# Attention products with V in one block per head, the sums by ones in another PSUM bank, and eleven query rows for every second key tile

## The chip, the cores and the metric

The kernel runs on one core of a Trainium2 chip. Its time is the device time of one execution in microseconds (us). Five engines work side by side, each through its own instructions in order, and wait for each other by semaphores: PE (TensorE, matrix products into PSUM), DVE (VectorE), ACT (ScalarE), POOL (GpSimd) and SP (which only issues DMAs here).

## The reference

One layer of a diffusion backbone on 1024 latent tokens, a grid of 16 rows and 64 columns, with 256 context tokens and a width of 1024. A modulated RMS norm is followed by one input projection. Half of its columns feed a neighbourhood attention of 8 heads of 64, the other half a gated short convolution. An output projection and a gated residual end the layer. What concerns the change is the attention:

```python
def neighbourhood_attention(q, k, v, kc, vc, rpb):
    ...
    wh = min(WIN_H, rows)                                    # 8 of 16 rows
    row_start = jnp.clip(qi - wh // 2, 0, rows - wh)
    row_idx = row_start[:, None] + jnp.arange(wh)[None, :]
    ...
    col_start = jnp.clip(cols - WIN_W // 2, 0, GRID_W - WIN_W)   # 16 of 64 columns
    ...
    s_lat = jnp.where(col_valid[:, None, :], s_lat, -jnp.inf)    # q_rot . k_rot * scale + bias
    s_ctx = jnp.einsum('biqhd,blhd->bhiql', q_plain, kc, ...) * scale
    s = jnp.concatenate([s_lat.reshape(*s_lat.shape[:4], n_lat), s_ctx], axis=-1)
    p = jax.nn.softmax(s, axis=-1).astype(v.dtype)
    o = (jnp.einsum('bhiqrk,birkhd->biqhd', p_lat, v_rows)
         + jnp.einsum('bhiql,blhd->biqhd', p_ctx, vc))
```

A query in row i sees the key rows from clip(i - 4, 0, 8) on, eight of them. So the keys of rows 0 to 7 are seen by query rows 0 to 11, and the keys of rows 8 to 15 by query rows 5 to 15.

## The kernel before

**Stages.** The norm and the modulation come first, then the projection of q, k and v by pairs of heads (PSUM tiles `pacc`), then the attention, and last the output projection (`pout`). The projections of the gates and of the convolution (`pu`) are cut into *ticks* of six 128x512 matmuls, and the attention uses them as a filling between its own work: 136 ticks in all, most of them in the attention.

**Key tiles and quarters.** A head's 1024 keys are 8 tiles of 128 (8 rows by 16 columns): tile j holds column group j // 2 and row half j % 2. A *quarter* is the pair of tiles 2g and 2g + 1, so a head has four, and the whole attention 32, numbered n = 4 h + g. Scores lie with the keys on the partitions and the queries along the row. A tile sees the query columns `span(j)`, which are 24, 31, 31 and 23 columns for g = 0 to 3, and by `seen` 12 query rows: 0 to 11 for even tiles, 4 to 15 for odd ones. `cells` cuts the same columns from the packed copy of the scores.

**One step of the loop**, `quarter(n)`, writes in this order:
- DVE: adds quarter n - 4's exponentials of the context keys to the head's running sums (`ctx_sum`) and quarter n - 5's of the latent keys (`lat_sum`, two instructions, one for each tile); then up to three chores of the filling.
- PE: the scores of quarter n into `sbank`, a tile of two PSUM banks (`pss`); the scores of the context keys of quarter n + 1 (`pc`), and between its two halves the transposes that bring maxima back to rows (`pmx<-ci,rm`).
- DVE adds the bias (`sb<-pss,bt`), which frees `sbank`; subtracts the maxima from quarter n - 3; ACT takes the exponentials.
- PE: one tick of filling, the transposes of the maxima of quarter n - 2 (`pmx<-ci,mx`), DVE's reduction of them (`rm`).
- PE, when o = n - 4 is the first quarter of a head or the last of all: the *block* of products with V (`weighted`), for the quarters since the last block, which are quarters 1, 2, 3 of one head and quarter 0 of the next. Then `total`: the head's sums over the partitions, as products with a column block of ones, into columns 384 to 511 of both banks of `sbank`.
- DVE: running maxima (`ctx_max`, `lat_max`); PE: the remaining ticks; ACT, after a block: `finish`, which copies the sums and the head's output out of PSUM and issues their DMAs.

The number of ticks of each step stands in the table `TICKS`, 36 numbers.

**The block.** An output `po` is one PSUM bank: partitions 0 to 63 hold the head's 64 channels for query columns 0 to 31, partitions 64 to 127 for columns 32 to 63. A product of V (128 keys by 64) with exponentials goes into one of the two halves; the two lists of products, one for each half, are issued alternately, wide ones first. A tile whose columns cross 32 is cut into two pieces. Per head each half has four latent products that are wide (288 or 276 columns), two narrow ones (96 or 84) and four of 256 columns with the context keys. `po` comes from the PSUM tag "O" with two buffers.

**What sets the order.** In the attention every engine's instructions are chained in the order in which the program writes them. After it the chaining ends (`strict[:] = []`), and a scheduler orders the loads, splits and matmuls of the output projection.

The lines that issue a block and the sums before:

```python
if live(o) and (o % 4 == 0 or final):
    weighted([m for m in range(o - 2 - (o % 4 == 0), o + 1) if live(m)])
    if o:
        hd_ = heads[(o - 1) // 4]
        hd_.total()
```

Of the kernel before, what the change touches and what calls it, by code (L numbers as in the profile page):

```python
# [19 lines left out]
P = 128  # L20
# [35 lines left out]
def body(tc, es, x, xb, xt, cb_, ct, w_mod, w_gate, b_ada, w_grp, w_col, q_g, k_g, bias, w_out, vecs, cst, out):  # L56
# [779 lines left out]
    def span(j):  # L836

        return max(j // 2 * 16 - 7, 0), min(j // 2 * 16 + 24, GW)

    def seen(v, j, cols=None):  # L840

        lo, hi = cols or span(j)
        return v.rearrange("p (c r) -> p c r", r=16)[:, lo:hi, 4 * (j % 2):4 * (j % 2) + 12]

    def cells(v, j, cols=None):

        at = span(j)
        lo, hi = cols or at
        return v[:, (lo - at[0]) * 12:(hi - at[0]) * 12].rearrange("p (c r) -> p c r", r=12)

    class head:
        def __init__(self, h):
# [45 lines left out]
            self.cps[g] = sc  # L898

        def scores(self, j, ps):  # L900
            q = seen(self.q[:, 0], j)
            for l in range(2):
                pe.matmul(cells(ps, j), self.k[:, j // 2, l, j % 2 * P:(j % 2 + 1) * P], q, start=(l == 0), stop=(l == 1))

        def lat_max(self, j, sb):
            m = seen(mx[:], j)
# [29 lines left out]

        def total(self):

            for i in range(2):
                for b in range(4):  # L940
                    at = 256 * b + 128 * i
                    pe.matmul(sbank[32 * b:32 * b + 32, i, 384:], onef, self.sum[:, at:at + 128], start=True, stop=True, skip_group_check=True)

        def finish(self):

            sums = ap.tile([P, 256], F32, name="sums", tag="sums", bufs=1)
            act.copy(sums[:].rearrange("p (r i c) -> p i r c", i=2, c=8), sbank[:, :, 384:].rearrange("p i (c r) -> p i r c", r=16))
            act.dma_start(rs_d[self.p][self.s].rearrange("b (x c) -> (b x) c", c=256),
                          sums[:].rearrange("(x o) c -> x o c", o=32)[:, 0])
            ob = ap.tile([P, 512], F32, name="ob", tag="ob", bufs=1)  # L950
            act.copy(blocked(ob[:]), self.po.rearrange("p (b c r) -> p b r c", b=2, r=16))
            for bank in range(2):
                act.dma_start(o_d[self.p][64 * self.s:64 * self.s + 64, bank * 512:(bank + 1) * 512], ob[64 * bank:64 * bank + 64])

    def pair_of(n):

        h, g = divmod(n, 4)
        return [(a, heads[h], 2 * g + a) for a in range(2)] if 0 <= h < NH else []
# [34 lines left out]
                     pm[:, 256:256 + nb * P].rearrange("p (i k) -> p i k", i=nb))  # L993
        return back

    def weighted(quarters):

        sides = [], []
        for m in quarters:
            for i, hd_, j in pair_of(m):  # L1000
                if j == 0:
                    hd_.po = psm.tile([P, 512], F32, name="po", tag="O", bufs=2)[:]
                for piece in hd_.pieces(j, sbs[m][:, i]):
                    sides[piece[0]].append((hd_, *piece))
            hd_ = heads[m // 4]
            for piece in hd_.ctx_pieces(m % 4):
                sides[piece[0]].append((hd_, *piece))
        for bank, side in enumerate(sides):
            side.sort(key=lambda piece: -piece[-1].free_size())
        for k in range(max(map(len, sides))):  # L1010
            for bank, side in enumerate(sides):
                if k < len(side):
                    hd_, _, j, dst, src = side[k]
                    pe.matmul(dst, hd_.v[:, j], src, start=(hd_, bank) not in opened, stop=k == len(side) - 1,
                              skip_group_check=True)
                    opened.add((hd_, bank))

    opened = set()

    def quarter(n):  # L1020

        live = lambda m: 0 <= m < 4 * NH
        ticks = TICKS[n]
        e, o = n - 3, n - 4
        final = o == 4 * NH - 1
# [24 lines left out]

        def biased():
            sb = sbs[n] = sb_new()
            bt = now[0][1].bt[:].rearrange("p v n -> p (v n)")[:, :1128].rearrange("p (a n) -> p a n", a=2)
            for at, slot, w_ in (((0, 31, 8), (8, 15, 16)), ((0, 0, 31),), ((0, 0, 31),), ((0, 0, 15), (15, 39, 8)))[n % 4]:
                dve.tensor_tensor(sb[:, :, at * 12:(at + w_) * 12], sbank[:, :, at * 12:(at + w_) * 12],
                                  bt[:, :, slot * 12:(slot + w_) * 12], ALU.add)

        if now and n >= 2:
            biased()
        if live(e):  # L1060
            heads[e // 4].ctx_exp(e % 4)
            w = both(sbs[e], e)
            w4 = w.rearrange("p a (c r) -> p a c r", r=12)
            dve.tensor_tensor(w4, w4, maxima_of(e), ALU.subtract)
            act.activation(w, w, AF.Exp)
        for _ in range(n > 0):
            next(fill, None)
        if 0 < n and n - 2 < 4 * NH:
            backs.append(maxima(n - 2))
        done = []  # L1070
        if live(o) and (o % 4 == 0 or final):
            weighted([m for m in range(o - 2 - (o % 4 == 0), o + 1) if live(m)])
            if o:
                hd_ = heads[(o - 1) // 4]
                hd_.total()
                done.append(hd_)
                if hd_.s:
                    ready.append(hd_.p)
# [347 lines left out]
```

## Time and profile before

| | before |
|---|---|
| median of 3 runs (lowest, highest) | 610.72 us (608.78, 611.19) |
| profiled execution, its own time | 609.24 us |
| its span | 607.5 us |
| mean granted clock of PE | 0.996 |
| PE busy | 594.1 us, 98% of the span |
| DVE, ACT, POOL busy | 401.5, 273.5, 66.3 us |
| from 258 to 502 us, the attention | PE busy 241.54 of 244 us, DVE 207.38, ACT 123.10 |

A row of the timeline gives the start in us, the time from the first start to the last end of the merged instructions, the engine, the line, the operation, what it writes and reads, the shape, the count, and in brackets how long the engine was idle before and what released it. Since nearly all instructions are issued through helper functions, their line is L71, and the tile names tell the groups apart. The end of a matmul in the profile is modelled and overlaps the next one's start, so the pace of matmuls is read from start to start. A product of 32-bit values without rounding (all products with V and with ones) stands in the trace as two records.

### The profile page before, as it was taken

How to read it: one execution, taken by the hardware profiler on the slowest of the kernel's cores; microseconds unless marked ns; L12 is line 12 of the kernel's file. 1: busy time of each engine (PE TensorE's matmuls, PEld its weight loads, DVE VectorE, ACT ScalarE, POOL GpSimd, SP SyncE). 2: the span in 40 equal slices, each digit the busy share in tenths (PEclk: the TensorE clock that was granted, in tenths of full speed). 3: DMA queues.
4: the chain of work that ended last, by engine and by line, in shares of the span. 5: the costliest groups of instructions: out<-in, count | busy, mean ns of one | idle time of the engine just before them, and what ended most of it. 6: DMA issues, size and time to landing. Idle time of an engine off the chain costs nothing.

```text
span 607.5 us, 9599 instructions
## 1 busy us (share of the span) xinstructions
PE 594.1 (98%) x3412; PEld 503.7 (83%) x3412; DVE 401.5 (66%) x833; ACT 273.5 (45%) x636; POOL 66.3 (11%) x86
## 2 busy tenths in 40 slices
PE   7799999999999999999999999999999999999998
PEld 3577899999999999888878787878787778888887
DVE  1476879646536555468999787999897785493201
ACT  6645355426526446334464464556455545360000
POOL 1001024123213222000000000000000002003200
PEclk9899999999999999999999999999999999999999
DMA  8995566734424673956264646546732227953631
GB/s 325 413 417 202 179 233 195 235 114 151 156 88 153 222 259 120 327 192 212 71 215 152 229 149 235 172 167 219 234 112 82 81 70 219 373 172 117 230 104 53
DMA packets 63227, 116.14 MB, mean 191 GB/s; under 512 B 7377, under 2 KB 26313, under 8 KB 60876
## 3 DMA queue, kind: packets, MB, share of 16 engines
q1 hardware_dynamic: 56684, 103.95, 49.5%
q10 hardware_dynamic: 6240, 11.05, 5.9%
q0 software_dynamic: 256, 0.54, 0.3%
q8 instruction: 27, 0.44, 0.3%
q14 instruction: 20, 0.16, 0.1%
HBM read 86.08 MB, written 29.43 MB: 190 GB/s over the span
## 4 chain that ended last, share of the span: by engine, by line
PE 94%; DMA 3%; DVE 1%; SPq 1%; ACT 0%; issue 0%
PE pu L71 31%; PE pacc L71 21%; PE po L71 6%; PE acc L71 5%; PE pout L92 5%; PE pout L90 5%; PE pout L91 5%; PE pss L71 4%; PE cacc L71 4%; DMA slab<-in_w_mod 3%; PE pc L71 2%; PE pmx L71 2%; PE tr L71 1%; PE trA L71 1%; PE trB L71 1%; SPq L71 0%
## 5 line engine op out<-in xcount | busy, mean ns | idle before, releaser
L71 PE MATMUL pu<-h,uh 128*128 128x512 f32 x544 | 172.2, 398 | 0.0
L71 PE MATMUL pacc<-w,h 128*128 128x384 f32 x768 | 138.9, 337 | 0.9 <-ACT ub L71 0.5
L71 PEld LDWEIGHTS pacc<-w,h 128*128 128x128 f32 x768 | 132.7, 188 | 1.8 <-ACT ub L71 0.9
L71 PEld LDWEIGHTS pu<-h,uh 128*128 128x128 f32 x544 | 97.3, 188 | 18.3 <-issue 1.0
L71 PE MATMUL pu<-h,ul 128*128 128x512 f32 x272 | 106.5, 392 | 0.0
L71 PEld LDWEIGHTS pu<-h,ul 128*128 128x128 f32 x272 | 51.1, 188 | 11.4
L71 POOL TENSOR_TENSOR ss<-ss,few 128x4 f32<-128x4 f32 (+1 forms) x40 | 41.2, 1030 | 126.3 <-DVE ss L71 126.1
L91 PE MATMUL pout<-wol,yh 128*128 128x512 f32 (+2 forms) x136 | 51.6, 379 | 0.0
L92 PE MATMUL pout<-woh,yl 128*128 128x512 f32 (+2 forms) x136 | 50.4, 379 | 0.0
L90 PE MATMUL pout<-woh,yh 128*128 128x512 f32 (+2 forms) x136 | 50.4, 379 | 0.0
L71 PE MATMUL acc<-h,w 128*128 128x512 f32 x144 | 38.2, 411 | 0.0
L71 ACT COPY mg<-pmx 128x256 f32<-128x256 f32 (+1 forms) x33 | 12.1, 367 | 57.4 <-PE pmx L71 42.8
L71 DVE TENSOR_REDUCE ss<-sq 128x4 f32<-128x260 f32 (+1 forms) x40 | 15.7, 393 | 28.4 <-ACT sq L71 28.3
L71 DVE TENSOR_TENSOR sb<-pss,bt 128x192 f32<-128x192 f32 (+3 forms) x48 | 27.7, 604 | 10.1 <-PE pss L71 10.1
L71 PEld LDWEIGHTS acc<-h,w 128*128 128x128 f32 x144 | 26.6, 194 | 8.7 <-ACT h L71 1.2
L71 ACT ACTIVATE sq<-pacc 128x256 f32<-128x256 f32 x32 | 12.4, 387 | 47.2 <-PE pacc L71 46.5
L71 DVE TENSOR_TENSOR sum<-sum,sb 128x372 f32<-128x372 f32 (+2 forms) x64 | 31.9, 498 | 2.0
L71 DVE TENSOR_TENSOR mx<-mx,sb 128x372 f32<-128x372 f32 (+2 forms) x64 | 31.8, 497 | 1.9
L71 ACT ACTIVATE qn<-pacc,ss 128x64 f32<-128x64 f32 x128 | 30.1, 330 | 4.9 <-PE trA L71 2.5
L71 ACT ACTIVATE sc<-sc 128x512 f32<-128x512 f32 x32 | 20.2, 633 | 21.6 <-DVE sc L71 21.6
L71 DVE TENSOR_TENSOR ul<-uraw,uh 128x512 fp32r<-128x512 f32 x34 | 23.0, 684 | 10.5 <-ACT uh L71 10.5
L91 PEld LDWEIGHTS pout<-wol,yh 128*128 128x128 f32 x136 | 25.6, 188 | 4.7
(141 smaller groups left out, 939.6 us busy)
## 6 DMA issues: line engine op xcount, KB each, us to landing
uraw<-in_w_col SPq DMA_DIRECT2D x34, 256.0 KB, 3.5
slab<-in_w_mod SPq DMA_DIRECT2D x8, 1024.0 KB, 9.6
q_d<-qs SPq DMA_DIRECT2D x32, 256.0 KB, 2.2
k_s<-k_d SPq DMA_DIRECT2D x8, 1024.0 KB, 7.6
q_s<-q_d SPq DMA_DIRECT2D x16, 512.0 KB, 4.9
wr<-in_w_grp SPq DMA_DIRECT2D x40, 192.0 KB, 2.4
bt<-in_rpb SPq DMA_DIRECT2D x8, 564.0 KB, 6.9
xn<-in_xb SPq DMA_DIRECT2D x8, 512.0 KB, 8.2
```

Source lines behind the costliest of these rows:

```text
L71: i = emit(*a, **kw)
L90: i = pe.matmul(ps, ah, bh, start=first, stop=False)
L91: pe.matmul(ps, ah, bl, start=False, stop=False)
L92: pe.matmul(ps, al, bh, start=False, stop=last)
```

## The change

It has three parts and a new table.

1. `weighted` takes one whole head. A block is written where o is the *last* quarter of a head (n = 4 h + 7), and has this head's four quarters. The block of quarter 0 of the first head alone, which stood at n = 4, is gone; there are 8 blocks, before there were 9.
2. `total` writes to a tile `ptot` of its own from the tag "O", as four products of 256 columns, before eight of 128 columns into `sbank`. `finish` copies from it.
3. `seen` and `cells` give odd tiles 11 query rows (5 to 15) in the maxima, the sums and the products with V. The scores are computed on 12 rows as before (`twelve`).

Since a block needs all the sums of its head, `lat_sum` is called for two quarters in the step of a block, for none in the step after it, and for one in the others. `TICKS` moves the step with few ticks from n % 4 = 0 to n % 4 = 3; its sum is 110 as before.

```diff
-TICKS = [2, 3, 3, 3, 2, 4, 4, 3] + 2 * [1, 4, 4, 4] + [2, 4, 4, 4] + 2 * [1, 4, 4, 3] + [1, 4, 4, 2] + [1, 3, 4, 3]
+TICKS = [2, 3, 3, 4, 4, 4, 4, 1] + [4, 4, 4, 1] + [4, 4, 4, 2] + [4, 4, 4, 1] + 3 * [4, 4, 3, 1] + [3, 2, 3, 1]
...
     def seen(v, j, cols=None):
 
         lo, hi = cols or span(j)
-        return v.rearrange("p (c r) -> p c r", r=16)[:, lo:hi, 4 * (j % 2):4 * (j % 2) + 12]
+        return v.rearrange("p (c r) -> p c r", r=16)[:, lo:hi, 5 * (j % 2):12 + 4 * (j % 2)]
+
+    def twelve(v, j):
+
+        lo, hi = span(j)
+        return v.rearrange("p (c r) -> p c r", r=16)[:, lo:hi, 4 * (j % 2):12 + 4 * (j % 2)]
...
-        return v[:, (lo - at[0]) * 12:(hi - at[0]) * 12].rearrange("p (c r) -> p c r", r=12)
+        return v[:, (lo - at[0]) * 12:(hi - at[0]) * 12].rearrange("p (c r) -> p c r", r=12)[:, :, j % 2:]
...
         def total(self):
 
-            for i in range(2):
-                for b in range(4):
-                    at = 256 * b + 128 * i
-                    pe.matmul(sbank[32 * b:32 * b + 32, i, 384:], onef, self.sum[:, at:at + 128], start=True, stop=True, skip_group_check=True)
+            self.tot = psm.tile([P, 512], F32, name="ptot", tag="O", bufs=2)
+            for b in range(4):
+                pe.matmul(self.tot[32 * b:32 * b + 32, :256], onef, self.sum[:, 256 * b:256 * b + 256], start=True, stop=True, skip_group_check=True)
...
-    def weighted(quarters):
-
+    def weighted(hd_):
+
+        hd_.po = psm.tile([P, 512], F32, name="po", tag="O", bufs=2)[:]
         sides = [], []
-        for m in quarters:
-            for i, hd_, j in pair_of(m):
-                if j == 0:
-                    hd_.po = psm.tile([P, 512], F32, name="po", tag="O", bufs=2)[:]
+        for m in range(4 * hd_.h, 4 * hd_.h + 4):
+            for i, _, j in pair_of(m):
                 for piece in hd_.pieces(j, sbs[m][:, i]):
...
-        for m in (o - 1, o)[:1 + final]:
+        for m in () if o % 4 == 0 else (o - 1, o) if o % 4 == 3 else (o - 1,):
             for i, hd_, j in pair_of(m):
                 hd_.lat_sum(j, sbs[m][:, i])
...
-        if live(o) and (o % 4 == 0 or final):
-            weighted([m for m in range(o - 2 - (o % 4 == 0), o + 1) if live(m)])
-            if o:
-                hd_ = heads[(o - 1) // 4]
-                hd_.total()
-                done.append(hd_)
+        if live(o) and o % 4 == 3:
+            hd_ = heads[o // 4]
+            weighted(hd_)
+            hd_.total()
+            done.append(hd_)
```

How the instructions stand. First PE before, at n = 4, the short block of the first head's quarter 0 between two ticks:

```order
L71 MATMUL pu<-h_251,ul 128x512
L71 MATMUL pmx<-ci,mx 128x128 x2
L71 MATMUL po<-sb,v_3055 64x24x12 x2
L71 MATMUL po<-sc,v_3055 64x256 x2
L71 MATMUL pu<-h_164,uh 128x512 x2
```

All four products go to the same half, and in the changed program nothing stands in their place. Next PE before, at n = 8, the end of the first long block, with the sums and the scores that follow (v_3055 is the first head's V; the block began with its last three quarters and the second head's first one, v_3056, mixed by width):

```order
L71 MATMUL po<-sc,v_3055 64x256
L71 MATMUL po<-sb,v_3055 64x7x12
L71 MATMUL po<-sb,v_3055 64x8x12
L71 MATMUL po<-sb,v_3055 64x7x12
L71 MATMUL po<-sb,v_3055 64x8x12
L71 MATMUL pss<-sum,onef 32x128 x8
L71 MATMUL pss<-q_s,k_s 128x372 x4
```

The sums by ones and the scores behind them write the same tile `pss`. And PE in the changed program, the first head's block at n = 7, in full:

```order
L71 MATMUL pmx<-ci,mx 128x128 x2
L71 MATMUL po<-sb,v_3055 64x24x12 x2
L71 MATMUL po<-sb,v_3055 64x23x12 x2
L71 MATMUL po<-sb,v_3055 64x24x11 x2
L71 MATMUL po<-sc,v_3055 64x256 x8
L71 MATMUL po<-sb,v_3055 64x23x11 x2
L71 MATMUL po<-sb,v_3055 64x7x12
L71 MATMUL po<-sb,v_3055 64x8x12
L71 MATMUL po<-sb,v_3055 64x7x11
L71 MATMUL po<-sb,v_3055 64x8x11
L71 MATMUL ptot<-sum,onef 32x256 x4
L71 MATMUL pss<-q_s,k_s 128x288 x4
```

As many products as before stand in the block, from one head, half of the latent ones narrower by a twelfth; scores follow the sums directly in both, before the second quarter of the same head (372 columns), now the first of the next (288). Last, DVE in the changed program at n = 11, around the start of the step of a block:

```order
L71 TENSOR_TENSOR mx<-mx,sb 128x31x11
L71 TENSOR_TENSOR sum<-sc 128x256
L71 TENSOR_TENSOR sum<-sum,sb 128x31x12
L71 TENSOR_TENSOR sum<-sum,sb 128x31x11
L71 TENSOR_TENSOR sum<-sum,sb 128x23x12
L71 TENSOR_TENSOR sum<-sum,sb 128x23x11
L71 TENSOR_TENSOR ul<-uraw,uh 128x512
L71 TENSOR_TENSOR sb<-pss,bt 128x2x180
```

Four sums over latent keys stand ahead of the bias there, before it were two in every step. Behind the last sums by ones PE has 60 matmuls `pu` (10 ticks) in the changed program and 66 (11 ticks) before; up to the first step of the attention, the instructions of every engine stand as they did.

More of the change, by code (lines that the diff above doesn't have):

```diff
@@ L900, in scores @@
         def scores(self, j, ps):
-            q = seen(self.q[:, 0], j)
+            q = twelve(self.q[:, 0], j)
             for l in range(2):
-                pe.matmul(cells(ps, j), self.k[:, j // 2, l, j % 2 * P:(j % 2 + 1) * P], q, start=(l == 0), stop=(l == 1))
+                pe.matmul(cells(ps, j - j % 2), self.k[:, j // 2, l, j % 2 * P:(j % 2 + 1) * P], q, start=(l == 0), stop=(l == 1))
         def lat_max(self, j, sb):
@@ L994, in maxima @@
         return back
-    def weighted(quarters):
+    def weighted(hd_):
+        hd_.po = psm.tile([P, 512], F32, name="po", tag="O", bufs=2)[:]
         sides = [], []
-        for m in quarters:
-            for i, hd_, j in pair_of(m):
-                if j == 0:
-                    hd_.po = psm.tile([P, 512], F32, name="po", tag="O", bufs=2)[:]
+        for m in range(4 * hd_.h, 4 * hd_.h + 4):
+            for i, _, j in pair_of(m):
                 for piece in hd_.pieces(j, sbs[m][:, i]):
-                    sides[piece[0]].append((hd_, *piece))
-            hd_ = heads[m // 4]
+                    sides[piece[0]].append(piece[1:])
             for piece in hd_.ctx_pieces(m % 4):
-                sides[piece[0]].append((hd_, *piece))
-        for bank, side in enumerate(sides):
+                sides[piece[0]].append(piece[1:])
+        for side in sides:
             side.sort(key=lambda piece: -piece[-1].free_size())
[L1010 to L1018, printed above, removed]
+        last = len(sides[0]) - 1
+        for k in range(last + 1):
+            for side in sides:
+                j, dst, src = side[k]
+                pe.matmul(dst, hd_.v[:, j], src, start=k == 0, stop=k == last, skip_group_check=True)
     def quarter(n):
@@ L1024, in quarter @@
         e, o = n - 3, n - 4
-        final = o == 4 * NH - 1
         left = do_frees(1) + 2 if n > 2 else 3
@@ L1070, in quarter @@
         done = []
[L1071 to L1078 removed]
+        if live(o) and o % 4 == 3:
[3 more added lines that the diff above has]
+            done.append(hd_)
+            if hd_.s:
+                ready.append(hd_.p)
         if now:
```

2 lines of the change are left out of this document (1 added, 1 removed).

## The prediction

> **What bounds the kernel now.** I read the page first, then a table of busy time by stage, the list of waits, and the timeline of PE around three blocks.
>
> ```profile
> PE 594.1 (98%) x3412; PEld 503.7 (83%) x3412; DVE 401.5 (66%) x833; ACT 273.5 (45%) x636; POOL 66.3 (11%) x86
> ...
> PE 94%; DMA 3%; DVE 1%; SPq 1%; ACT 0%; issue 0%
> ```
>
> PE is busy for 98% of the span and carries 94% of the chain that ends last. The table by stage has the stretch, then the busy time of PE, PEld, DVE, ACT and POOL:
>
> ```profile
> 72.00:258.00 186.00, 186.00 (x1078) 178.12 (x1076) 112.06 (x282) 87.79 (x314) 46.89 (x51) 1.00 0.57 189
> 258.00:502.00 244.00, 241.54 (x1494) 196.16 (x1493) 207.38 (x405) 123.10 (x214) 0.27 (x4) 1.00 0.49 162
> 502.00:604.60 102.60, 102.59 (x471) 85.98 (x469) 42.90 (x68) 23.15 (x38) 13.64 (x14) 1.00 0.56 187
> ```
>
> From 72 us to the last matmul PE has no gap except 2.46 us in the attention (244 less 241.54). So a product less there shortens the kernel by its own time, and what DVE or ACT save is worth nothing until PE waits for them. The list of waits, asked for PE in this stage alone, has one row (us in all, times, the longest):
>
> ```profile
> PE pss L71 <- ACT sums L71: 2.5, 5, 0.5
> ```
>
> Five times the scores waited for ACT's copy of the sums, which lie in the same tile. The timeline of PE shows the short block, a tick behind maxima without a block, and the first long block:
>
> ```profile
> 281.62 0.38 PE L71 MATMUL pmx<-ci,mx 128*128 128x128 f32 x2
> 281.93 1.19 PE L71 MATMUL po<-sb,v 128*64 128x288 f32 x4
> 282.95 1.03 PE L71 MATMUL po<-sc,v 128*64 128x256 f32 x4
> 283.90 0.74 PE L71 MATMUL pu<-h,uh 128*128 128x512 f32 x2
> 284.48 0.40 PE L71 MATMUL pu<-h,ul 128*128 128x512 f32 x1
> ...
> 288.17 0.38 PE L71 MATMUL pmx<-ci,mx 128*128 128x128 f32 x2
> 288.31 0.71 PE L71 MATMUL pu<-h,uh 128*128 128x512 f32 x2
> 288.86 0.40 PE L71 MATMUL pu<-h,ul 128*128 128x512 f32 x1
> ...
> 308.15 2.12 PE L71 MATMUL po<-sb,v 128*64 128x288 f32 x16
> 310.10 1.90 PE L71 MATMUL po<-sc,v 128*64 128x256 f32 x16
> 311.83 0.50 PE L71 MATMUL po<-sb,v 128*64 128x84 f32 x8
> 312.26 0.64 PE L71 MATMUL pss<-sum,onef 128*32 128x128 f32 x16
> 313.39 0.95 PE L71 MATMUL pss<-q_s,k_s 128*128 128x372 f32 x4 [0.49 <-ACT sums L71]
> ```
>
> The reader is to see three things. The 16 records of 256 columns take 310.10 to 311.83, 1.73 us, and in the short block 4 of them take 0.95 us: in a long block the two halves run beside each other, in the short one, with everything in one half, they run one by one. So a long block costs its longer half: 2 records of each product, 8 x 256 columns in 1.73 us, 0.845 ns for a column. And the scores start 1.13 us after the sums.
>
> **The change part by part.** *The short block goes.* From its maxima to the next tick are 2.28 us (281.62 to 283.90); where no block stands there, it is 0.14 us (288.17 to 288.31). The first pair of the tick takes 0.58 us behind the block and 0.55 us behind maxima. PE saves 2.14 + 0.03 = **2.17 us**. Its products don't come back: the long blocks stay eight and as long as they were, since the last one was lopsided already and took the full time with 30 records, where the others have 40:
>
> ```profile
> 496.31 4.11 PE po L71 x30
> ...
> 500.99 15.19 PE pu L71 x66
> 516.17 1.59 PE pout L90 x7
> ```
>
> (This is the chain of waits in order of time; 308.15 to 312.26 is 4.11 us too.)
>
> *Eleven rows.* In each half of a block one product of 288 columns becomes 264, one of 276 becomes 253, and one of 96 becomes 88 (84 becomes 77 beside it): 55 columns less in the longer half. Twice, since each is two records, at 0.845 ns: 0.093 us a head, **0.74 us** in all. The price of a run of 11 columns, which starts at an odd place, no row shows. The nearest rows are the runs of 12 at a step of 16 (the 16 records of 288 and 276) against the unbroken 256. The former have (4 x 288 + 4 x 276) = 2256 columns in 1.95 us, 0.864 ns each with the block's start in them, 2% over the unbroken ones. I take no surcharge; the bounds are the whole 0.74 us lost (a run of 11 priced as 12) and, far on the other side, the odd products at twice their time, which is a rival below.
>
> The Trainium skill says on this, in "PSUM — Partial Sum Buffer", Specifications (TRN2), that PSUM has lines of 8 bytes and that any access pattern with gaps slows matmuls significantly. The runs of 12 have gaps too and pay the 2%; by the page the change would keep or raise that price, by the rows it loses nothing.
>
> *The sums by ones.* Eight products of 128 columns become four of 256. Column for column that is the same work, and I take 0. From the sums to a following tick is 0.57 us (below), so the bounds are a tenth of that either way for each head, 0.5 us in all.
>
> *The wait goes.* Where a tick follows the sums, the step is shorter:
>
> ```profile
> 484.06 0.64 PE L71 MATMUL pss<-sum,onef 128*32 128x128 f32 x16
> 484.63 0.73 PE L71 MATMUL pu<-h,uh 128*128 128x512 f32 x2
> ```
>
> 0.57 us against 1.13 us, five times: 5 x 0.56 = **2.80 us**. In the changed program the scores don't touch the tile of the sums, and what else they need is long there. The next head's K and Q are asked for one and two steps before the block's step, and no wait of PE for them is in the list. The bounds are 0 (another wait ends as late) and 2.80. `ptot` comes from the tag of `po`: two buffers for `po`, `ptot`, `po`, `ptot` in turn, so each finds one whose content was copied a whole head ago.
>
> *DVE's four sums.* In the step of a block two more sums stand ahead of the bias. Their price and the nearest deadline, in the tightest steady step that I find (DVE, then PE):
>
> ```profile
> 420.64 0.41 DVE L71 TENSOR_TENSOR mx<-pc,sc 128x256 f32<-128x256 f32 x1
> ...
> 422.13 0.92 DVE L71 TENSOR_TENSOR sum<-sum,sb 128x276 f32<-128x276 f32 x2
> ```
> ```profile
> 422.90 0.40 PE L71 MATMUL pc<-q_s,kc_s 128*128 128x256 f32 x2
> 423.13 0.38 PE L71 MATMUL pmx<-ci,rm 128*128 128x128 f32 x2
> ```
>
> The next context scores (422.90) need the buffer that the maximum at 420.64 reads until 421.05: 1.85 us of room. Two sums of 276 columns take 0.92 us, so 0.9 us stay. The step ahead of them has a lighter one before it (no sums of latent keys at all in the step behind a block), so DVE doesn't run up a debt. I take 0. If that cover were gone, each of the eight blocks would wait for what is missing, at most the 0.92 us.
>
> *DVE's narrower maxima and sums* save a twelfth of instructions like the 0.92 us pair on an engine that PE doesn't wait for: 0. *The moved ticks* are 110 before and after; 12 or so stand between blocks in both: 0.
>
> *The last stage.* One tick less lies between the last block and the output projection, 15.19 / 11 = 1.38 us. That is cover for the first loads of the last stage. What is late there first is the seventh column group's y: ACT rounds its second half and DVE takes the rest, and PE uses them:
>
> ```profile
> 522.56 0.63 ACT L1317 CAST yh<-tb 128x512 fp32r<-128x512 f32 x1 [4.60 <-DMA tb<-y_d]
> ```
> ```profile
> 523.22 0.69 DVE L1318 TENSOR_TENSOR yl<-tb,yh 128x512 fp32r<-128x512 f32 x1 [4.53 <-ACT yh L1317]
> ```
> ```profile
> 524.40 0.39 PE L90 MATMUL pout<-woh,yh 128*128 128x512 f32 x1
> ...
> 525.08 0.39 PE L92 MATMUL pout<-woh,yl 128*128 128x512 f32 x1
> ```
>
> Room is 524.40 - 523.19 = 1.2 us. But the loads hang on the ticks (ACT's queue stands behind the second-last unit of the filling, and behind the last convolution, both counted back from the start of the output projection), not on the block. I take 0, with 1.4 us as the bound.
>
> *Sum:* 2.17 + 0.74 + 2.80 = 5.71 us. The profiled execution took 609.24 us, its span 607.5 and 1.7 around it; it becomes 603.5. The median, 610.72, lies 1.5 above that execution, so I predict **605.0 us**. Its own range, from the bounds of the small terms and the spread of the three runs (608.78 to 611.19), is 603.2 to 606.8.
>
> **The rivals.**
>
> *The wait only changes its name.* The scores behind a block are now a head's first, and they or the maxima behind them could be held by something that ends as late as the copy did. For it: the five waits were 0.49 us, small enough to have hidden another. Against it: the list has no other row. The gain is then 2.17 + 0.74 = 2.91 us: 607.8.
>
> *DVE becomes the bound in the step of a block.* For it: DVE is busy for 207 of 244 us here, and the room was 1.85 us in a step of three ticks, which the new table keeps for the last heads. Against it: the light step behind. If DVE comes 0.92 us too late at seven blocks, 6.4 us, it takes all: 611.4, no change. If half of that, 608.2.
>
> *The last stage starves.* Up to 1.4 us at the first late load: 606.4. If ACT's queue is pushed back at more than one load, twice that, 607.8.
>
> *Rows of eleven are dear (slower).* Runs of 44 bytes that begin at a multiple of 4 bytes may cost PE or its writes more than the runs of 12 do. Per head and half the odd products have 264 + 253 + 88 = 605 columns; at twice the time that is 2 x 605 x 0.845 ns = 1.02 us, 8.2 us for eight heads. The change then ends at 605.0 + 8.2 = 613.2. It is slower than before from a surcharge of 5.71 / 8.2, 70%, on. Against it stands the 2% of the runs of 12. It is what the page on PSUM quoted above warns of, if the slowing there grows with the oddness of the run.
>
> *The change doesn't do what it says* can't be a rival: the order of instructions has the eight blocks, the narrower products and the sums in `ptot`.
>
> **How the numbers follow.** My forecast has 0.77; the wait that changes its name 0.07; DVE 0.06; the last stage 0.06; the dear rows of eleven 0.04. The bound of "no change" is 0.5%, 3.05 us, about what a measurement of this kernel can tell: faster is below 607.67, slower above 613.77. The forecast's range lies in faster nearly whole (0.75), of the last stage 0.05, of the wait and of DVE 0.02 each: 0.84. Slower takes a part of the rows of eleven and the spread of the measurements: 0.03. The rest, 0.13, is no change. The range that should hold the time 8 times in 10 goes from 602.8 to 607.9: the forecast's own, a little under it for the runs' spread, and up to the case of the wait and the last stage.
>
> **What would show it.** In the profile after: no wait of PE for ACT's copy of the sums, and 0.57 us or so from the sums to the scores; eight blocks of about 4.02 us (4.11 less 0.09), nothing of `po` before 290 us; PE's gap in the attention near zero, and the attention shorter by 5.7 us, while the stages before it are as long as they were. Odd products should take as much less as they have columns less, 11 of 12. What would make it wrong: an odd product as long as an even one or longer, a new wait of PE for DVE within a step behind a block, or PE idle between 515 and 530 us for y or the output weights.

## The result: slower by half a per cent, and the profile after

The changed kernel took 615.01 us (median of 5 executions, 613.38 to 615.36). The ratio to the kernel before is 1.0058, with a 95% interval of 1.0032 to 1.0084. A second measurement of the same kernel gave 613.15 us (12 executions) and 1.0044, 1.0028 to 1.0061. The forecast was 605.0 us and faster. The first profiled execution took 613.38 us, its span is 611.4.

The page of the changed kernel, PE's busy time and the chain that ended last:

```profile
PE 594.8 (97%) x3347; PEld 501.1 (82%) x3348; DVE 400.3 (65%) x833; ACT 273.1 (45%) x636; POOL 66.3 (11%) x86
...
PE 80%; DMA 7%; DVE 6%; ACT 3%; issue 2%; ACTq 1%; SPq 0%; POOL 0%; DVEq 0%; POOLq 0%
```

PE carried 94% of the chain before, now 80%. The busy times by stage (stretch; its length; PE, PEld, DVE, ACT and POOL busy) say where:

```profile
72.00:258.00 186.00, 185.56 (x1073) 177.54 (x1072) 113.24 (x284) 87.35 (x313) 46.86 (x51) 1.00 0.56 187
258.00:502.00 244.00, 238.94 (x1411) 193.25 (x1411) 205.31 (x406) 122.66 (x211) 0.27 (x4) 1.00 0.48 163
```

PE idles for 5.06 us from 258 to 502 us, before for 2.46. What for stands in its list of waits (us in all, times, the longest):

```profile
PE pmx L71 <- ACT mg L71: 4.2, 4, 1.9
...
PE pmx L71 <- DVE rm L71: 0.8, 1, 0.8
...
PE pu L71 <- ACT zs L71: 0.5, 1, 0.5
...
PE pout L90 <- ACT yh L1313: 0.2, 1, 0.2
```

The row of before, scores behind ACT's `sums`, is gone. The new first row is the transposes of the maxima (`pmx<-ci,mx`), behind ACT's copy `mg`, which takes maxima that were brought back to rows out of PSUM. The timeline of PE around the fifth head's block, the worst place (start, duration, what, idle before and releaser; heads are counted from 1 here and in the expectations):

```profile
423.11 1.62 PE L71 MATMUL po<-sb,v 128*64 128x288 f32 x12
424.55 1.90 PE L71 MATMUL po<-sc,v 128*64 128x256 f32 x16
426.28 0.91 PE L71 MATMUL po<-sb,v 128*64 128x253 f32 x12
427.12 0.64 PE L71 MATMUL ptot<-sum,onef 128*32 128x256 f32 x8
427.69 0.81 PE L71 MATMUL pss<-q_s,k_s 128*128 128x288 f32 x4
...
430.18 0.39 PE L71 MATMUL pu<-h,ul 128*128 128x512 f32 x1
432.47 0.44 PE L71 MATMUL pmx<-ci,mx 128*128 128x128 f32 x2 [1.90 <-ACT mg L71]
```

The two savings in these rows came as priced: the block takes 4.01 us (423.11 to 427.12), and the scores follow the sums by 0.57 us. Then the scores, the context scores and a tick run through, and the maxima of the next step wait 1.9 us.

What `mg` waited for is on ACT's own queue. First ACT in the changed kernel, then in the kernel before, both behind the block of the fifth head (ACTq rows are DMA issues):

```profile
427.83 0.37 ACT L71 COPY sums<-ptot 128x256 f32<-128x256 f32 x1 [0.82 <-PE ptot L71]
428.18 0.59 ACT L71 COPY ob<-po 128x512 f32<-128x512 f32 x1
429.69 0.53 ACTq L952 DMA_DIRECT2D rs_d<-sums  x1
430.60 1.35 ACTq L957 DMA_DIRECT2D o_d<-ob  x2
432.04 0.37 ACT L71 COPY mg<-pmx 128x256 f32<-128x256 f32 x1 [3.28 <-DMA rb<-ri_d]
```
```profile
430.10 0.37 ACT L71 COPY sums<-pss 128x256 f32<-128x256 f32 x1 [2.09 <-PE pss L71]
430.37 0.59 ACT L71 COPY ob<-po 128x512 f32<-128x512 f32 x1
430.50 0.53 ACTq L948 DMA_DIRECT2D rs_d<-sums  x1
431.13 1.67 ACTq L953 DMA_DIRECT2D o_d<-ob  x2
432.89 0.37 ACT L71 COPY mg<-pmx 128x256 f32<-128x256 f32 x1 [1.93 <-DVE sb L71]
```

Between the copies and `mg` stand `finish`'s three DMA issues. Before, the first left 0.13 us after the start of `ob`, and `mg` ended at 433.26, 0.14 us ahead of PE's transposes:

```profile
433.40 0.38 PE L71 MATMUL pmx<-ci,mx 128*128 128x128 f32 x2
```

In the changed kernel the first issue stood for a microsecond and a half and the others followed late, 4.2 us from `sums` to `mg` instead of 2.8. In the list of ACT's waits three of the seven blocks stand out, those of heads 3, 5 and 6, and the releaser is a DMA each time:

```profile
ACT mg L71 <- DMA y_d<-tb: 3.5, 1, 3.5
ACT mg L71 <- DMA rb<-ri_d: 3.3, 1, 3.3
...
ACT mg L71 <- DMA o_d<-ob: 2.1, 1, 2.1
```

Why a store of 4 KB should wait for other transfers is told by the instructions of the built program. Each DMA of SP and ACT tells of its landing by a semaphore of a set of eight that are handed out in turn (the trace has 50 DMAs on each of the eight), and a DMA that takes a semaphore waits until the DMA before it on that semaphore has landed, as a rule the one eight issues earlier. Here are the rows of SP and ACT (number on its engine, name, what it waits for) around the fifth head's block:

```
273 L867 DMA k_s_4869<-k_d3_86 128x1x2048 [waits DMAHW6_49]
274 L319 DMA uraw_4780<-in_w_col 128x512 [waits DMAHW7_49,DVE_49]
275 L530 DMA rb_4728<-ri_d1_96 64x512 [waits DMAHW0_49,DVE_49]
...
280 L881 DMA v0_3055<-v_d3_90 128x640 [waits DMAHW5_49,PE_49]

472 L952 DMA rs_d2_73<-sums_4718 4x256 [waits DMAHW6_49,Activation_49]
473 L957 DMA o_d2_59<-ob_4721 64x512 [waits DMAHW7_49,Activation_49]
474 L957 DMA o_d2_59<-ob_4721 64x512 [waits DMAHW0_49]
```

The store of the sums has the semaphore of the next head's K. SP's timeline and part 6 of the page (KB each, median us to landing) put times to it:

```profile
422.78 0.71 SPq L867 DMA_DIRECT2D k_s<-k_d  x1
```
```profile
k_s<-k_d SPq DMA_DIRECT2D x8, 1024.0 KB, 7.1
```

The trace has K's landing at 429.62, 6.8 us after its issue, and the store left at 429.69. The two issues behind it left 0.08 and 0.02 us after the landings of `uraw` and `rb`, which had the semaphore before them, and at head 3 the two stores of the output left 0.08 and 0.04 us after those of `rb` and `y_d`. Before, K was issued at 419.37 and ten DMAs ahead of the store, which followed one from 420.78; that had landed at 429.17, and the store left at 430.50. Of the 24 issues of the kernel before none left less than 0.2 us after the landing that it needed. The block moved a step ahead, into the landing of the next head's loads.

That is heads 3 and 5. At heads 1 and 6 PE waits too (0.5 and 0.7 us), but the landings that the issues needed were 5 to 18 us old. There one issue took long by itself: 1.08 us at head 1, as in the kernel before, and 1.41 us at head 6, where 0.46 to 0.61 us are usual; why isn't shown. It becomes a stall because the room is gone everywhere, as at head 4, where no issue is held or long. First the kernel before, then the changed one:

```profile
402.02 0.37 ACT L71 COPY sums<-pss 128x256 f32<-128x256 f32 x1 [2.15 <-PE pss L71]
404.23 0.37 ACT L71 COPY mg<-pmx 128x256 f32<-128x256 f32 x1 [1.35 <-PE pc L71]
405.31 0.38 PE L71 MATMUL pmx<-ci,mx 128*128 128x128 f32 x2
```
```profile
400.29 0.37 ACT L71 COPY sums<-ptot 128x256 f32<-128x256 f32 x1 [0.61 <-PE ptot L71]
402.50 0.37 ACT L71 COPY mg<-pmx 128x256 f32<-128x256 f32 x1 [1.35 <-PE pc L71]
402.93 0.44 PE L71 MATMUL pmx<-ci,mx 128*128 128x128 f32 x2
```

ACT needs 2.21 us from `sums` to `mg` in both. Before, `mg` ended 0.71 us ahead of PE's transposes, now 0.06 us ahead of transposes that just waited for it. The scores' wait of 0.56 us, which the change removed, was cover for ACT's three issues, and so was the longer first product of scores (372 columns, now 288).

### The profile page after: what moved, and what is told of

It reads as the page before. It is cut to its first block, busy times and chain, and to the rows that moved or that the text cites. A ratio compares the mean times of both kernels' runs of the same rounds, so it can differ in the third digit from the quotient of the medians.

```text
span 611.4 us, 9460 instructions
## 1 busy us (share of the span) xinstructions
PE 594.8 (97%) x3347; PEld 501.1 (82%) x3348; DVE 400.3 (65%) x833; ACT 273.1 (45%) x636; POOL 66.3 (11%) x86
## 4 chain that ended last, share of the span: by engine, by line
PE 80%; DMA 7%; DVE 6%; ACT 3%; issue 2%; ACTq 1%; SPq 0%; POOL 0%; DVEq 0%; POOLq 0%
PE pu L71 24%; PE pacc L71 21%; PE acc L71 5%; PE po L71 4%; PE pout L90 4%; PE pout L92 4%; PE pout L91 4%; PE cacc L71 4%; DMA rb<-ri_d 3%; PE pss L71 2%; PE tr L71 2%; PE pmx L71 2%; PE pc L71 2%; DMA woraw<-in_w_out 2%; DMA xn<-in_xb 1%
## 5 line engine op out<-in xcount | busy, mean ns | idle before, releaser
L90 PEld LDWEIGHTS pout<-woh,yh 128*128 128x128 f32 x136 | 25.6, 188 | 5.7 <-ACT yh L1313 1.1
L92 PEld LDWEIGHTS pout<-woh,yl 128*128 128x128 f32 x136 | 25.6, 188 | 5.1 <-DVE yl L1314 0.4
```

The lines of the kernel that those rows point to most:

```text
L90: i = pe.matmul(ps, ah, bh, start=first, stop=False)
L92: pe.matmul(ps, al, bh, start=False, stop=last)
```

## The experiments

All kernels are alike up to the first scores. These start anywhere from 257.3 to 261.4 us in the 14 profiles, the kernel before among the early ones at 258.0 (its issue with SP at 258.3). So beside the times the table has the stretch from the first scores to the end of the span, which leaves that chance out. That column is of one profiled execution each, and two of the changed kernel differ by 2.5 us in it; so differences of 1 us or less between kernels are read from steps and waits, not from it.

| kernel | median us (executions) | ratio to before, 95% | first scores to end, us |
|---|---|---|---|
| before | 609.1 to 610.7 (5 series) | | 349.42 |
| changed | 615.01 (5) | 1.0058, 1.0032 to 1.0084 | 352.16 |
| changed, again | 613.15 (12) | 1.0044, 1.0028 to 1.0061 | 354.64 |
| e1_sp | 606.42 (10) | 0.9943, 0.9925 to 0.9962 | 345.22 |
| e2_late | 607.36 (10) | 0.9965, 0.9946 to 0.9983 | 346.27 |
| e3_two | 611.11 (10) | 1.0024, 0.9994 to 1.0054 | 352.57 |
| e4_bank | 613.65 (10) | 1.0067, 1.0045 to 1.0088 | 354.17 |
| part1 | 613.52 (10) | 1.0061, 1.0037 to 1.0086 | 353.24 |
| gate1 | 614.09 (7) | 1.0062, 1.0039 to 1.0085 | 352.07 |
| b_sp | 609.09 (10) | 1.0000, 0.9976 to 1.0024 | 349.49 |
| sp_bank | 608.32 (10) | 0.9976, 0.9956 to 0.9996 | 348.50 |
| sp_twelve | 606.97 (10) | 0.9960, 0.9931 to 0.9988 | 345.98 |
| sp_tail | 605.31 (7) | 0.9937, 0.9917 to 0.9958 | 345.79 |
| best | 605.46 (7) | 0.9932, 0.9902 to 0.9963 | 344.40 |

### The issues off ACT's queue, or behind mg

```diff
-            act.dma_start(rs_d[self.p][self.s]..., sums...)
+            sp.dma_start(rs_d[self.p][self.s]..., sums...)
...
-                act.dma_start(o_d[self.p]..., ob...)
+                sp.dma_start(o_d[self.p]..., ob...)
```

> The changed kernel, with the three DMAs behind each block (sums to rs_d, the head's output to o_d) issued by SP, not by ACT. Theory A (ACT's queue): in the step behind a block the transposes of the maxima on PE wait for ACT's copy mg, and mg stands behind these DMA issues (head 3: 3.2 us of them, head 5: 2.3, head 6: 2.1). Then PE's waits for mg fall from 4.2 us to under 1, the attention from the first scores to the last product with ones from 244.8 us to 239 to 240.5, and the time from 615 to 608.5 to 610.5. Rival B (DVE's sums in the block's step, or its longer order): nothing changes, 614 to 616. Rival C (only the start and the last stage differ): 614 to 616 with the attention at 244.8.

Theory A holds; the time came out below its range. At the same head ACT goes from the copies to `mg` in 0.29 us, and SP does the standing (the timeline of ACT and SP, head 5):

```profile
425.94 0.37 ACT L71 COPY sums<-ptot 128x256 f32<-128x256 f32 x1 [0.86 <-PE ptot L71]
426.21 0.59 ACT L71 COPY ob<-po 128x512 f32<-128x512 f32 x1
427.09 0.37 ACT L71 COPY mg<-pmx 128x256 f32<-128x256 f32 x1 [0.29 <-ACT ob L71]
```
```profile
426.25 0.32 SPq L1221 DMA_DIRECT2D zs<-z_d  x1
428.69 0.53 SPq L952 DMA_DIRECT2D rs_d<-sums  x1
```

The store still waits until 428.69, but behind it on SP nothing is urgent. PE's list has no wait for `mg` any more, and in the attention a single row:

```profile
PE pmx L71 <- DVE rm L71: 0.4, 1, 0.4
```

Six microseconds (0.9943 against 1.0044) hang on which engine issues 24 DMAs. The second form leaves them on ACT, behind `mg` and the context scores' copy of the next step:

```diff
+            def send():
+                mark = act.last
+                def put(dst, src):
+                    behind(act.dma_start(dst, src), mark)
...
+        if sends:
+            sends.pop()()
```

> The changed kernel, with the same three DMAs left on ACT's queue but issued in the next step, behind its copies mg and sc; the copies of sums and output stay where they were. Theory A (the issues are what is in the way): as with SP, waits for mg under 1 us, attention 239 to 240.5 us, time 608.5 to 610.5; the gates of a pair begin one step later. Rival A2 (the two copies, 1.3 us, are in the way already): about half of the 4.2 us of waits stays, 612 to 613.5. Rivals B and C: 614 to 616.

`mg` is free here too, and PE doesn't wait for it. So the issues were in the way and not the copies, and here too the time is below the range of Theory A. (The edit also begins the work on a finished pair one step later; the run gate1 below does that alone, and the stalls stay.) It is 1 us slower than with SP, by the medians and from the first scores to the end, probably because the issues now stand ahead of the exponentials (at head 5 ACT is idle for 3.93 us before them), and PE waits 0.4 us for `sb`.

Does the edit alone do it? The same on the kernel before:

> The kernel before, with its three DMAs behind each block issued by SP. It tells whether the gain of the same edit on the changed kernel belongs to the change or to the edit alone. Theory A: in the kernel before, PE's maxima never waited for mg, and the five waits of the scores are for the copy of the sums, which stands ahead of the DMAs: nothing to gain, 609 to 611, the attention from first scores to last sums at 242.2 to 243. Rival: ACT's queue was a hidden cost before too: 607 or less. It is also a second look at the start: the first projection product stood at 67.1 us before and at 67.9 to 69.1 in the five changed kernels; if that is chance, it will lie among these here.

It gains nothing. PE waits for `sums` as before:

```profile
PE pss L71 <- ACT sums L71: 2.6, 5, 0.5
```

### More cover, and the transfers of the gates

```diff
-        for _ in range(n > 0):
+        first = (n > 0) + (n > 4 and o % 4 == 0)
+        for _ in range(first):
             next(fill, None)
```

> The changed kernel, with two ticks, not one, ahead of the maxima's transposes in the step behind a block; the step's number of ticks is kept. Theory A: 1.38 us more cover; of the stalls of 0.5, 1.15, 1.9 and 0.7 us about 0.5 us is left, attention 240 to 241, time 609.5 to 611. If ACT's queue were so late that the wait is not bounded by one tick: 612. Rival B (DVE late): the maxima come to DVE 1.4 us later and the stall appears at the next pmx<-ci,rm or context scores, 614 to 617.

The stalls at heads 1 and 6 are gone, those at heads 3 and 5 are not:

```profile
PE pmx L71 <- ACT mg L71: 2.7, 2, 1.9
PE pmx L71 <- DVE rm L71: 1.5, 1, 1.5
PE pu L71 <- ACT zs L71: 1.2, 1, 1.2
```

At head 5 the first issue left 2.1 us later than in the changed kernel, though `sums` started only 0.4 later, and the added tick was eaten by it (ACT's timeline):

```profile
428.22 0.37 ACT L71 COPY sums<-ptot 128x256 f32<-128x256 f32 x1 [0.80 <-PE ptot L71]
428.57 0.59 ACT L71 COPY ob<-po 128x512 f32<-128x512 f32 x1
431.83 0.53 ACTq L952 DMA_DIRECT2D rs_d<-sums  x1
```

So a tick of cover was enough at heads 1 and 6, where no issue was held, and not at heads 3 and 5, where the wait hangs on a transfer. At head 5 the first issue waited for K, which was issued 0.5 us later than in the changed kernel and took 8.5 us, not 6.8; why wasn't followed. The attention took 246.1 us, where Theory A had 240 to 241, and the last maxima come to PE later (`rm` 1.5). The profiled execution was a long one (614.23 us, the median is 611.11), so these stalls may be above the usual.

The next run begins the work on a finished pair one step later:

```diff
+        if live(o) and o >= 4 and o % 8 == 0:
+            ready.append(o // 8 - 1)
...
-            if hd_.s:
-                ready.append(hd_.p)
...
+            if o == 4 * NH - 1:
+                ready.append(hd_.p)
```

> The changed kernel, DMAs still on ACT's queue, but the work on a finished pair (the loads of its sums and outputs, its y) begins one step later, as it stood to the next head's loads before the change. PE's order is the same. If it is these transfers that the issues behind a block wait for (y at head 3, the reciprocals' broadcast at head 5), these two stalls shrink, waits for mg under 2 us, 609.5 to 612.5. If it is the next head's loads alone, or the number of transfers in flight whatever they are, the waits stay at 4 us or move to other heads, 613 to 615.5.

Mixed. At head 3 the stall is gone, where the changed kernel's releaser was y, and at head 6 nearly so. At head 5 it grew to 2.7 us, and another DMA (`z_d`) had the semaphore there:

```profile
PE pmx L71 <- ACT mg L71: 3.2, 2, 2.7
```

The times are the changed kernel's. Which transfer holds an issue changes with the order of the queue. The sum of the waits for `mg` fell from 4.2 and 5.0 us to 3.2, not below the 2 us that were expected if y and the reciprocals were all.

### Which part of the change brings it

```diff
-            self.tot = psm.tile([P, 512], F32, name="ptot", tag="O", bufs=2)
-            for b in range(4):
-                pe.matmul(self.tot[32 * b:32 * b + 32, :256], onef, self.sum[:, 256 * b:256 * b + 256], ...)
+            for i in range(2):
+                for b in range(4):
+                    at = 256 * b + 128 * i
+                    pe.matmul(sbank[32 * b:32 * b + 32, i, 384:], onef, self.sum[:, at:at + 128], ...)
```

> The changed kernel with the sums by ones back in the scores' second bank (eight products of 128), all else as changed. By the forecast's step (the wait of the scores costs 0.56 us each, nothing stands behind it): six blocks are followed by scores, 3.4 us more than the changed kernel, 618 to 619. Theory A (the wait only moved to the maxima): the scores wait 0.5 us at six places again, and the maxima's waits for mg shrink by nearly as much, from 4.2 to about 2 us: 0.5 to 1.5 us more than the changed kernel, 615 to 616.5.

Here Theory A's second half fell. The waits for `sums` came back, and the waits for `mg` stayed beside them, in a list of PE for the attention:

```profile
PE pmx L71 <- ACT mg L71: 3.4, 3, 2.3
PE pss L71 <- ACT sums L71: 2.5, 5, 0.5
```

The ticks, in whose steps the stalls lie, take 160.94 us against 160.86 in the changed kernel, while the sums take 2.95 more. At heads 1, 3 and 5 the steps ahead of the maxima lose 3.9 us, in the changed kernel 4.0. So the wait was not simply handed on from the scores to the maxima; only head 6's stall of 0.7 us is gone, and heads 2 and 4 have 0.5 us of room again. Since two profiles of the changed kernel differ by 2.2 us in the ticks, a part handed on isn't excluded. (The wait for `sums` occurs five times, not six as I wrote: behind the blocks of heads 3, 7 and 8 come ticks.) The times, with intervals of a quarter of a per cent, can't tell 2 to 3 us here.

The edit above and 12 rows for odd tiles (the diff stands with sp_twelve) leave the first part and its table alone in place:

> The changed kernel with its second and third part undone: sums by ones in the scores' bank and 12 rows for odd tiles. What stays is the block of one whole head, a step earlier, with the new table; the DMAs are on ACT's queue. Theory (the earlier block puts its DMA issues among the transfers for the next head, whatever the other parts do): PE waits for mg 3.5 to 5 us, the ticks take as long as in the changed kernel, the attention 248 to 249 us, 615 to 617. Rival (the eleven rows or the sums' bank bring the stalls): waits for mg under 1 us, 610 to 612.

PE waits for `mg` at three blocks, 2.9 us in all, a little under what the theory had, like the attention (246.6 us) and the time:

```profile
PE pmx L71 <- ACT mg L71: 2.9, 3, 1.5
```

The rival (waits under 1 us, 610 to 612) is out. The stalls at heads 1, 3 and 5 come with the earlier block and its table, whatever is done with the sums and the rows; the one at head 6 is absent here and in e4_bank, and so needs the sums in `ptot` or is chance. No run parts the earlier block from the table.

### The disputed terms, with ACT's queue free

The sums in the scores' bank, with the DMAs on SP:

> The changed kernel with the DMAs on SP, and the sums by ones back in the scores' second bank. Theory A (with the queue of ACT free, the forecast's price of the wait holds, 0.56 us at each of six blocks that scores follow): 3.4 us more than with SP alone, 609.5 to 610.2; PE waits for ACT's sums 0.5 us six times, for mg not at all. Rival (the wait is worth little because something else ends as late): less than 1 us more, 606.5 to 607.4.

PE waits 2.6 us for `sums`, five times. From the first scores to the end 348.50 against 345.22 us: 3.3 us, where 0.56 us at five places is 2.8; the steps of the sums alone took 3.0 us more, and 0.2 of the rest lies in the output stage. The median, 608.32 us, lies between the two ranges, 1.9 us above SP alone. The forecast's price of the wait holds by the steps.

```diff
-        return v.rearrange("p (c r) -> p c r", r=16)[:, lo:hi, 5 * (j % 2):12 + 4 * (j % 2)]
+        return v.rearrange("p (c r) -> p c r", r=16)[:, lo:hi, 4 * (j % 2):12 + 4 * (j % 2)]
...
-        return ....rearrange("p (c r) -> p c r", r=12)[:, :, j % 2:]
+        return ....rearrange("p (c r) -> p c r", r=12)
```

> The changed kernel with the DMAs on SP, and 12 rows for odd tiles again in maxima, sums and products with V. The forecast's step: a block 4.11 us, not 4.02, 0.74 us more in all, 607.2. Rival (rows of eleven dear): as fast as with SP alone or faster, 606.4 or less, with a block no longer than 4.02 us.

With 12 rows the block of head 5 takes 4.10 us in the timeline of PE:

```profile
419.11 2.12 PE L71 MATMUL po<-sb,v 128*64 128x288 f32 x16
...
423.21 0.64 PE L71 MATMUL ptot<-sum,onef 128*32 128x256 f32 x8
```

With 11 it took 4.01. The products with V take 0.60 us more in all than with SP alone, and from the first scores to the end it is 0.76 us, of which 0.2 lies in the output stage; 0.74 was forecast for the products. The medians (606.97 and 606.42) lean the same way within their intervals.

### Two waits at the end

```diff
-... + [3, 2, 3, 1]
+... + [3, 3, 2, 1]
```

> The changed kernel with the DMAs on SP, and the last four steps with 3, 3, 2, 1 ticks instead of 3, 2, 3, 1. With SP alone PE waits 0.4 us for DVE's last reduction of maxima, which has two ticks of cover; here it has three. Expected: that wait gone, 0.4 us less than with SP alone, 606.0, which the times can hardly tell but the list of waits can. If the wait were DVE's running late by more than a tick, it stays.

The wait for `rm` is gone, but a tick less stands ahead of the last block, and that waits for its last exponentials:

```profile
PE po L71 <- ACT sb L71: 0.8, 1, 0.8
```

The next takes the tick from the first step of the last head:

```diff
-... + 3 * [4, 4, 3, 1] + [3, 2, 3, 1]
+... + 2 * [4, 4, 3, 1] + [3, 4, 3, 1] + [3, 3, 3, 1]
```

> The changed kernel with the DMAs on SP, and one tick moved from the first step of the last head (4 to 3) to the last but two (2 to 3): three ticks of cover for the last reduction of maxima, as in the run with 3, 3, 2, 1, and three again ahead of the last block, which there had two and waited 0.8 us for the last exponentials. Expected: PE waits neither for DVE's rm nor for the last sb; what stays is zs, 0.5 us. Time 605 to 606.5, ratio to before 0.992 to 0.995. If DVE is late in the shorter step, a new wait of up to 1 us there.

Both waits are gone; the one that is left stands behind the last sums:

```profile
PE pu L71 <- ACT zs L71: 0.5, 1, 0.5
```

605.46 us, 0.9932 of the kernel before (0.9902 to 0.9963), 5.0 us less from the first scores to the end. It beats both kernels; the times don't tell it from sp_tail and e1_sp.

And the changed kernel once more:

> The changed kernel unchanged, a second profile and a closer time. Expected: 613 to 615.5; waits of PE for mg 3.5 to 5 us at the same heads (1, 3, 5, 6), so that they belong to the program and not to one execution. Open is the last stage: in the first profile it took 92.6 us from the first output product to the end and PE waited for yh, in every other kernel 91.5; if that is chance, it is 91.5 here and the time nearer 613.

The second profile has the same four blocks and 5.0 us of waits for `mg`, and the last stage took 92.7 us again. So both belong to the program and not to one execution.

## Why the prediction was wrong, step by step

Steps of PE from start to start, added up by kind from the first scores to the last product with ones, in us. A wait lies in the step ahead of it, so stalls of the maxima stand in the ticks' row.

| kind | before | changed | DMAs on SP |
|---|---|---|---|
| products with V | 34.84 | 32.23 | 32.26 |
| products with ones | 7.20 | 4.25 | 4.24 |
| transposes of maxima, mx | 5.67 | 5.81 | 5.47 |
| scores, context scores, transposes rm | 41.57 | 41.62 | 41.62 |
| ticks (records) | 153.41 (654) | 160.86 (660) | 155.22 (660) |

- **The short block and the eleven rows** were to save 2.17 + 0.74 = 2.91. The products with V lost 2.60 in either kernel, and the step at the short block's maxima 0.20 (5.67 to 5.47): 2.80. Right. A row of eleven has no surcharge: 0.09 us a block, as the columns say. The Trainium skill's warning on patterns with gaps ("PSUM — Partial Sum Buffer", Specifications (TRN2)) has no effect that this case could see beyond the 2% of the runs of 12.
- **The sums and the wait of the scores** were to save 2.80. The steps of the sums lost 2.96. Right, and sp_bank gives it back.
- **The moved ticks: 0** failed: it is the step that put the earlier block behind other transfers and gave that no price. The ticks took 7.45 us more; the one tick that now lies ahead of the last block (6 records of 0.23) is 1.4 of it and comes off behind it, and the other 6 are longer steps: 4.9 ahead of maxima that wait for `mg`, 1.0 ahead of the last reduction `rm` (8 in all in the second profile, where the ticks took 163.1). *What else they need is long there* was right for the scores, which ran through, but the forecast stopped at them and at DVE. It didn't follow the moved step's own DMAs on ACT, nor ask what stood covered by the wait that it removed. The room could be read before: `mg` ended 0.7 us ahead of PE at heads 2, 4 and 6 and 0.14 us ahead at head 5, and 0.56 us of it came from that wait. Without it any delay of the issues is a stall.
- **The rival "the wait only changes its name"** had the place right ("the maxima behind them") and the size wrong. It was capped at the loss of the 2.80. The new wait isn't simply the old one handed on: with the old one back, in e4_bank, it stays at heads 1, 3 and 5. It is set by the landings and the issues, and has no such cap. 7 in 100 was too little for it, and no rival priced ACT's queue in the attention.
- **DVE** was given 0 and had it, but for one place at the end: the last reduction `rm` held PE for 0.8 us, 0.4 with SP.
- **The last stage** was given 0 with a bound of 1.4. Behind the last sums PE waits 0.4 to 0.6 us for `zs` in every kernel with the new table, and in the changed kernel the output stage took 92.57 and 92.69 us, before 91.44: most of it ahead of products with y's first halves (`yh`), whose loads ACT issues too. The other ten kernels with the new block had 91.4 to 91.8. So 1.1 to 1.3 of the loss is here, and with the 0.9 below the stages behind the attention lost 2.0, over the bound. Why the output stage is longer in this kernel alone wasn't tried.

The account of the changed kernel, first scores to end: -2.60 of the products, -2.95 of the sums, +6.1 of stalls among the ticks, +0.2 of other steps in the attention, +0.9 between the last sums and the output stage beside the moved tick, +1.1 in the output stage: +2.7, as measured (349.42 to 352.16). With the DMAs on SP the same sum without the stalls is -4.2, and -5.0 in the best version; the forecast was -5.7. The rest of that gap is `rm`, `zs` and the slower steps around them.

What was shown by runs: that the issues on ACT's queue make the stalls (two ways of moving them), that the earlier block with its table brings most of them (part1), that the same edit gains nothing without the change (b_sp), and that the other two terms are worth what was forecast. Read from the instructions' semaphores and the landings in the traces, and not tried by itself, is that at heads 3 and 5 the issues wait for an earlier DMA on the same semaphore. Why the issues were not held in the kernel before rests on that reading. Why single issues took long at heads 1 and 6 stays open.

## What to carry to other kernels

A DMA that a computing engine issues is an instruction in that engine's order, with waits of its own. When a step moves, list every DMA that it issues, find what each must wait for where it now stands, and what on the same engine is behind it; room of 0.1 us is no room. When a wait is removed, ask what it gave cover to. If the queue's other work is on the critical path, issue from an engine that has nothing urgent behind it.

## What the runs showed of the hardware that I had not expected

- An issue that isn't allowed to go holds its engine: 3.3 us of idle ACT at head 5, 3.5 at head 3, with copies ready behind it. The Trainium skill has the first half in "Perfetto Trace Analysis", DMA Instruction — HWDGE (DVE, Sync): the wait for semaphores is the issuing sequencer's, and the reported start comes after it. The rows agree: the store of the sums starts at 429.69 and ACT is idle ahead of it. In "DMA: Bandwidth & Descriptors", Issuing engines are not separate DMA queues, the Trainium skill says that issuing from several engines saves only the time to initiate a DMA, usually small beside the DMA itself. Here the choice of the issuing engine was worth 1.0044 against 0.9943, a full per cent, because ACT stood for the issues and their waits ahead of `mg`; so the measurement says more than the page.
- The start varied by 4 us: the first scores stood at 257.3 to 261.4 us in 14 profiles of kernels that are alike up to there. A difference of half a per cent is better looked for from a mark behind the start.
- Runs of 11 columns that begin at an odd place cost PE no more than the columns they have: 4.01 against 4.10 us for the block of head 5.
